# Index scores of a sparse-attention block: the low part of the keys in row halves of TensorE, two heads at a time

## The chip, the cores and the metric

The kernel runs on one core of a Trainium2 chip. The metric is the device time of one execution in microseconds, the median of three runs. The profile is one more execution, taken by the hardware profiler.

## The reference

A hybrid block on 2048 positions of width 1024: an input projection, an RWKV-7 recurrence as one branch, sparse attention as the other, both gated, merged and normed. The change touches the index scores of the sparse branch. For every query (in blocks of 128) 8 index heads of width 64 score all earlier keys, and the 256 best keys are kept:

```python
s_idx = jax.nn.relu(jnp.einsum('bqhd,bsd->bqhs', qi_b, ki))
score = jnp.einsum('bqh,bqhs->bqs', wi_b, s_idx).astype(jnp.float32)
score = jnp.where(causal[None], score, -jnp.inf)
_, sel = lax.top_k(score, topk)
```

The keys `ki` are the same for all heads; `wi` weighs the heads. The choice of keys has to be exact enough in float32, so the kernel works with numbers split in two: a high part `hi`, rounded to the form that TensorE multiplies, and a low part `lo`, the rest.

## The kernel before, in words

`build` (from L1207) states the stages in this order, each with a priority band (a smaller number goes first): `start` (norm and transposes), `gemm_index` (L277, index queries, keys and head weights), `select` (L372, index scores and choice of keys), `gemm_half` for the first two of four blocks of 512 tokens, then the recurrence (`rwkv_open`, `rwkv_pass`, `rwkv_inv`, `rwkv_chain`) with `gemm_half` for the other two blocks around it, `heads`, `branch_a`, `attention`, `finish`. A planner orders each engine's instructions ahead of time, with a simulated timeline: an instruction of a lower band is placed where nothing of a higher one is ready. So the products of `gemm_half` (all made at L251 by `unit`) fill TensorE between the score matmuls of `select`. On the chip each engine then takes its instructions in that fixed order.

`gemm_index` makes the index queries 128 rows (two heads) at a time. `split_out` (L255) writes their high and low parts, and `stacked` (L269) stores them by four transfers on SyncE's queue (issued at L75 by `move`) into `QIS`, an array of 8 heads by 128 rows: rows 0 to 63 of a head are its high part, rows 64 to 127 its low part. `stacked` is used for the attention queries `QS` too. The keys' two parts go to `KIH`.

`select` loads the keys into two tiles `kim`: `M[0]` holds the high part twice, in rows 0 to 63 and again in 64 to 127, and `M[1]` the low part twice. It goes through five groups of query blocks, (14, 15), (11, 12, 13), (8, 9, 10), (5, 6, 7), (2, 3, 4); blocks 0 and 1 need no choice. For each block it loads the queries of all heads as `st` (128 rows, 8 heads, 128 queries) and goes over the keys in chunks of at most 1024 columns and over the 8 heads. A head's scores for a chunk are a tile `ixs` of 128 by 1024, two banks of PSUM; there are three such tiles in turn. In cuts of at most 512 columns, two matmuls (L423) go into it: `st[:, h]` with `M[0]` and with `M[1]`. As `st` holds high and low one above the other, the two give (hi + lo) times the high keys and (hi + lo) times the low keys, all four products. Each matmul has its own weight load (the page calls the loads PEld). ScalarE then takes the tile out with a ReLU (L425, tile `re`, two of them) and VectorE adds it, weighed, to the block's scores (L429 for the first head, L431). Behind that, statistics and eight counting passes find the threshold (L434 to L471), and the mask goes to memory (L492 to L501).

After the choice of keys the recurrence begins. It has matmuls with operands of 64 rows, so of half the array's height: L654 and L659 (low part of two small weights, in rows 0 to 63 and 64 to 127, each right behind a whole one, L653 and L658) and L703 (four matmuls in the lower half of the rows, then four in the upper). Its last matmuls are those of L808.

Of the kernel before, what the change touches and what calls it, by code (L numbers as in the profile page):

```python
# [24 lines left out]
FT = mybir.dt.float32  # L25
# [26 lines left out]
class Block:  # L52
# [216 lines left out]
    def stacked(self, dst, p, m, tb, scale=None):  # L269
        DMA = self.nc.sync  # L270
        hi, lo = self.split_out(p, scale)
        s = slice(tb * TB, (tb + 1) * TB)
        for hh in range(2):
            self.move(dst[2 * m + hh, 0:64, s], hi[hh * 64:hh * 64 + 64])
            self.move(dst[2 * m + hh, 64:128, s], lo[hh * 64:hh * 64 + 64])

    def gemm_index(self):  # L277
        nc = self.nc
# [93 lines left out]
    def select(self):  # L372
# [7 lines left out]
        V, A, T, G, DMA = nc.vector, nc.scalar, nc.tensor, nc.gpsimd, nc.sync  # L380
        MID = TOPK - 4.0
        with ExitStack() as ctx:
            k1 = self.pool("ix1", 1, side="right", ctx=ctx)
            w = self.pool("ixw", 2, side="right", ctx=ctx)
            ps = self.pool("ixp", 3, PSUM, ctx=ctx)
            M = [k1.tile([128, S], FR, name=f"kim{i}") for i in range(2)]
# [13 lines left out]
            for grp in self.groups:  # L400
# [4 lines left out]
                def sm(name, n=4, dt=FT, bufs=2):  # L405
                    return w.tile([128, n], dt, name=name, bufs=bufs)

                s1, s2, t, cnt = sm("s1"), sm("s2"), sm("t", bufs=3), sm("cnt", bufs=3)
                mean, inv = sm("mean"), sm("inv")
                for g, qb in enumerate(grp):  # L410
                    n, n1 = 128 * (qb + 1), 128 * qb
                    st = w.tile([128, 8, 128], FR, name="st")
                    self.move(st, self.QIS[:, :, qb * 128:(qb + 1) * 128].rearrange("h p q -> p h q"))
                    sco = w.tile([128, S], FT, name="sc", bufs=6)
                    sc.append(sco)
                    for k0 in range(0, n, 1024):
                        kn = min(1024, n - k0)
                        for h in range(8):
                            p = ps.tile([128, 1024], FT, name="ixs")
                            for a in range(0, kn, 512):  # L420
                                b = min(a + 512, kn)
                                for i in range(2):
                                    T.matmul(p[:, a:b], st[:, h], M[i][:, k0 + a:k0 + b], start=i == 0, stop=i == 1)  # L423
                            r = w.tile([128, 1024], FT, name="re")
                            A.activation(r[:, :kn], p[:, :kn], AF.Relu)  # L425
                            wi = self.wi[:, qb, h:h + 1]
                            o = sco[:, k0:k0 + kn]
                            if h == 0:
                                V.tensor_scalar(o, r[:, :kn], wi, None, op0=OP.mult)  # L429
                            else:  # L430
                                V.scalar_tensor_tensor(o, r[:, :kn], wi, o, op0=OP.mult, op1=OP.add)  # L431
                    V.tensor_tensor(sco[:, n1:n], sco[:, n1:n], tri, op=OP.add)

                    j = w.tile([128, S], BF, name="ja", bufs=1)  # L434
                    A.activation(j[:, :n1], sco[:, :n1], AF.Copy, accum_out=s1[:, g:g + 1])
                    V.tensor_scalar(mean[:, g:g + 1], s1[:, g:g + 1], -1.0 / n1, None, op0=OP.mult)
                    j = w.tile([128, S], BF, name="ja", bufs=1)
                    A.activation(j[:, :n1], sco[:, :n1], AF.Abs, bias=mean[:, g:g + 1], accum_out=s2[:, g:g + 1])
                    V.scalar_tensor_tensor(t[:, g:g + 1], s2[:, g:g + 1], zc[:, qb, 0:1], mean[:, g:g + 1],
                                           op0=OP.mult, op1=OP.subtract)  # L440
                    V.tensor_tensor(inv[:, g:g + 1], s2[:, g:g + 1], zc[:, qb, 1:2], op=OP.mult)
                hs = [w.tile([128, S], BF, name="hs", bufs=4) for _ in grp]
                told = cold = None
                for it in range(self.passes):
                    if it:
# [15 lines left out]
                        told, cold, t, cnt = t, cnt, tn, sm("cnt", bufs=3)  # L461
# [16 lines left out]
                p = ps.tile([128, 1024], FT, name="ixs")  # L478
# [898 lines left out]
```

## Time and profile before

| | |
|---|---|
| median of three runs | 2543.67 us |
| the three runs | 2540.09, 2543.67, 2544.42 us |
| the profiled execution | 2535.82 us |
| its span, first to last instruction | 2534.0 us |
| mean granted TensorE clock | 0.987 |
| TensorE matmuls busy | 2414.3 us (95%) |
| TensorE weight loads busy | 2134.6 us (84%) |
| VectorE, ScalarE, GpSimd busy | 1615.2, 1235.3, 804.8 us |

Times in the profile count from the span's start. PE is TensorE's matmuls, PEld its weight loads, which run beside the matmuls; DVE is VectorE, ACT ScalarE, POOL GpSimd, SP SyncE. A matmul's duration holds the way through the array, so matmuls overlap, and what one costs is read from start to start. "128\*128 128x512" is a weight of 128 rows by 128 columns and a moving operand of 128 rows by 512 columns. "Idle before" is the time in which the engine stood still ahead of an instruction; "issue" as its cause means that no semaphore of another engine explains it. The index scores and the choice of keys lie between 215 and 840 us.

### The profile page before, as it was taken

Reading aid. Unit: us, or ns where it says so; the run is one execution under the profiler, and the core shown is the slowest. Engines: PE = TensorE matmul, PEld = TensorE weight load, DVE = VectorE, ACT = ScalarE, POOL = GpSimd, SP = SyncE. Lnnn points to the kernel's source line nnn. Section 1 sums busy time; section 2 is a strip of 40 time slices with the busy share of each in tenths; the row PEclk is TensorE's granted clock in tenths of the full one; section 3 lists DMA queues with packets and bytes.
Section 4 is the critical chain, followed back from the end, with each engine's and each line's share of the span. In section 5 each row is a group of like instructions: output and inputs, shape, how many; then the busy total and the mean of one; then the engine's idle time right before and its main releaser. Section 6 shows DMA issues by size and latency. Waiting matters only on the chain.

```text
span 2534.0 us, 44949 instructions
## 1 busy us (share of the span) xinstructions
PE 2414.3 (95%) x16776; PEld 2134.6 (84%) x16776; DVE 1615.2 (64%) x3381; ACT 1235.3 (49%) x2024; POOL 804.8 (32%) x694
## 2 busy tenths in 40 slices
PE   4899999999999999999999999999889999989998
PEld 3687878888888998889888989989779999988887
DVE  6614778776877556654936757344478888876443
ACT  4414646555544424334434333352478888865332
POOL 2411111111121333233333332131255555544332
PEclk9999999999999999999999999999999999999999
DMA  7754223423336556777677769978753343155442
GB/s 248 280 152 125 89 83 92 125 96 96 104 98 217 147 164 193 191 203 225 194 206 212 214 188 276 298 240 250 232 166 87 91 118 99 29 182 192 142 150 71
DMA packets 423496, 415.67 MB, mean 164 GB/s; under 512 B 80010, under 2 KB 339890, under 8 KB 418404
## 3 DMA queue, kind: packets, MB, share of 16 engines
q1 hardware_dynamic: 422692, 404.33, 53.1%
q0 software_dynamic: 576, 8.39, 0.8%
q8 instruction: 132, 2.16, 0.4%
q14 instruction: 96, 0.79, 0.1%
HBM read 254.04 MB, written 160.15 MB: 163 GB/s over the span
## 4 chain that ended last, share of the span: by engine, by line
PE 49%; DMA 7%; DVE 5%; issue 3%; ACT 2%; SPq 2%; POOL 2%; POOLq 0%; ACTq 0%; DVEq 0%
PE g L251 16%; PE fo L1196 6%; PE yv L993 4%; PE br L1111 4%; PE pt L976 3%; PE pg L703 2%; PE lg L959 2%; PE lg L960 2%; DMA xt<-in_w_pb_dram 1%; PE pp L808 1%; PE pp L791 1%; PE zu L797 1%; PE hp L801 1%; PE pp L788 1%; DVE prd L740 1%
## 5 line engine op out<-in xcount | busy, mean ns | idle before, releaser
L251 PE MATMUL g<-hh,whi 128*128 128x256 f32 (+1 forms) x2176 | 718.9, 330 | 8.8 <-DVE eo L265 4.7
L251 PE MATMUL g<-hl,whi 128*128 128x256 f32 (+1 forms) x2176 | 715.3, 329 | 2.9 <-POOL hl L169 2.9
L251 PE MATMUL g<-hh,wlo 128*128 128x256 f32 (+1 forms) x2176 | 714.9, 329 | 1.4 <-POOL wlo L237 1.4
L237 POOL TENSOR_TENSOR wlo<-wraw,whi 128x1024 fp32r<-128x1024 f32 (+1 forms) x89 | 225.1, 2529 | 748.3 <-ACT whi L236 695.0
L251 PEld LDWEIGHTS g<-hh,whi 128*128 128x128 f32 x2176 | 416.0, 191 | 54.7 <-issue 6.5
L251 PEld LDWEIGHTS g<-hl,whi 128*128 128x128 f32 x2176 | 416.2, 191 | 43.4 <-issue 4.1
L251 PEld LDWEIGHTS g<-hh,wlo 128*128 128x128 f32 x2176 | 416.0, 191 | 41.7 <-issue 4.3
L431 DVE SCALAR_TENSOR_TENSOR sc<-re,wi,sc 128x1024 f32<-128x1024 f32 (+7 forms) x154 | 170.7, 1108 | 56.7 <-ACT re L425 50.8
L425 ACT ACTIVATE re<-ixs 128x1024 f32<-128x1024 f32 (+7 forms) x176 | 140.4, 816 | 135.5 <-PE ixs L423 78.7
L236 ACT CAST whi<-wraw 128x1024 fp32r<-128x1024 f32 (+1 forms) x89 | 92.8, 1043 | 174.2 <-PE g L251 132.3
L976 PE MATMUL pt<-ident,lt 128*128 128x128 f32 x1088 | 168.1, 275 | 7.0 <-ACT tp L982 4.3
L966 ACT ACTIVATE lt<-lt,nm 128x128 f32<-128x128 f32 (+15 forms) x128 | 154.8, 1212 | 15.3 <-DVE nm L965 15.2
L987 DVE TENSOR_TENSOR pl<-pt,ph 128x512 fp32r<-128x512 f32 (+1 forms) x216 | 139.0, 657 | 31.6 <-ACT ph L986 30.7
L423 PE MATMUL ixs<-kim,st 128*128 128x512 f32 (+3 forms) x608 | 150.2, 373 | 8.3 <-ACT re L425 4.8
L962 DVE CUSTOM_DVE_ANT_0 lt<-lg,mask 128x512 f32<-128x512 f32 (+3 forms) x256 | 147.4, 589 | 16.5 <-PE lg L960 9.0
L993 PE MATMUL yv<-ph,vp 128*128 128x256 f32 (+1 forms) x576 | 152.1, 285 | 5.7 <-ACT ph L986 5.6
L993 PE MATMUL yv<-pl,vp 128*128 128x256 f32 x576 | 153.0, 301 | 2.0 <-POOL pl L984 1.8
L959 PE MATMUL lg<-m,sq 128*128 128x256 f32 (+3 forms) x384 | 136.6, 365 | 5.9 <-DMA mask<-mask 4.1
L423 PEld LDWEIGHTS ixs<-kim,st 128*128 128x128 f32 x608 | 113.1, 190 | 34.5 <-ACT re L425 6.9
L976 PEld LDWEIGHTS pt<-ident,lt 128*128 128x128 f32 x1088 | 125.7, 141 | 16.9 <-ACT tp L982 5.3
L986 ACT CAST ph<-pt 128x512 fp32r<-128x512 f32 (+1 forms) x216 | 116.4, 564 | 20.8 <-PE pt L976 14.3
L960 PE MATMUL lg<-m,sq 128*128 128x256 f32 (+3 forms) x384 | 126.2, 336 | 0.0
(343 smaller groups left out, 5106.6 us busy)
## 6 DMA issues: line engine op xcount, KB each, us to landing
wraw<-in_w_in_dram SPq DMA_DIRECT2D x88, 512.0 KB
gg<-eo SPq DMA_DIRECT2D x64, 256.0 KB
gmd<-gt SPq DMA_DIRECT2D x64, 256.0 KB
gmc<-gmd SPq DMA_DIRECT2D x32, 512.0 KB
g<-gg SPq DMA_DIRECT2D x64, 256.0 KB
m<-ks SPq DMA_DIRECT2D x32, 512.0 KB
pj<-eo SPq DMA_DIRECT2D x52, 256.0 KB
x<-in_ada_w_dram SPq DMA_DIRECT2D x24, 512.0 KB
```

The costliest lines, as they stand in the source:

```text
L237: nc.gpsimd.tensor_tensor(lo[:, :, :n], raw[:, :, :n], hi[:, :, :n].bitcast(FT), op=OP.subtract)
L251: T.matmul(p[:, s], a[:, k], b[:, k, s], start=n == 0, stop=n == 3 * KD - 1)
L423: T.matmul(p[:, a:b], st[:, h], M[i][:, k0 + a:k0 + b], start=i == 0, stop=i == 1)
L425: A.activation(r[:, :kn], p[:, :kn], AF.Relu)
L431: V.scalar_tensor_tensor(o, r[:, :kn], wi, o, op0=OP.mult, op1=OP.add)
L959: T.matmul(p[:, :kn], sq[:, qb * 128:(qb + 1) * 128], m1[:, k0:k1_], start=True, stop=False)
L960: T.matmul(p[:, :kn], sq[:, qb * 128:(qb + 1) * 128], m2[:, k0:k1_], start=False, stop=True)
L962: V.tensor_tensor_reduce(lt[:, k0:k1_], p[:, :kn], mk, 1.0, -3.0e38, OP.subtract, OP.max, cm[:, i:i + 1])
L966: ex = A.activation(lt[:, :n], lt[:, :n], AF.Exp, bias=nm, accum_out=lsum[:, qb, h:h + 1])
L976: T.transpose(p[:, o:o + 128], L[i][:, kt * 128:(kt + 1) * 128], self.ident)
L993: T.matmul(yv[:, qs], vp[:, kt, :], b[:, o:o + nn], start=kt == 0 and i == 0, stop=kt == last and i == 1, skip_group_check=True)
L1196: T.matmul(p, a[:, k, q], b[:, k, s], start=n == 0, stop=n == 23)
```

## The change

`stacked` stores odd heads of `QIS` with the low part in rows 0 to 63 and the high part in rows 64 to 127; even heads, and `QS`, are as before. `select` takes two heads at a time and two tiles `ixs` at once. First come the whole passes with the high keys, for the one head over all cuts, then for the other. Then, cut by cut, each head's high queries with the low keys, 64 rows: rows 0 to 63 for the even head, rows 64 to 127 for the odd one. The product of low with low is no longer made. ReLU and the weighed sum are unchanged.

```diff
         hi, lo = self.split_out(p, scale)
         s = slice(tb * TB, (tb + 1) * TB)
         for hh in range(2):
-            self.move(dst[2 * m + hh, 0:64, s], hi[hh * 64:hh * 64 + 64])
-            self.move(dst[2 * m + hh, 64:128, s], lo[hh * 64:hh * 64 + 64])
+            for i, t in enumerate((hi, lo)):
+
+                o = 64 * (i ^ (hh if dst is self.QIS else 0))
+                self.move(dst[2 * m + hh, o:o + 64, s], t[hh * 64:hh * 64 + 64])
...
                     for k0 in range(0, n, 1024):
                         kn = min(1024, n - k0)
+                        cuts = [(a, min(a + 512, kn)) for a in range(0, kn, 512)]
                         for h in range(8):
-                            p = ps.tile([128, 1024], FT, name="ixs")
-                            for a in range(0, kn, 512):
-                                b = min(a + 512, kn)
-                                for i in range(2):
-                                    T.matmul(p[:, a:b], st[:, h], M[i][:, k0 + a:k0 + b], start=i == 0, stop=i == 1)
+                            if h % 2 == 0:
+
+                                pp = [ps.tile([128, 1024], FT, name="ixs") for i in range(2)]
+                                for i, p in enumerate(pp):
+                                    for a, b in cuts:
+                                        T.matmul(p[:, a:b], st[:, h + i], M[0][:, k0 + a:k0 + b], start=True, stop=False)
+                                for a, b in cuts:
+                                    for i, p in enumerate(pp):
+                                        r_ = slice(i * 64, i * 64 + 64)
+                                        T.matmul(p[:, a:b], st[r_, h + i], M[1][r_, k0 + a:k0 + b], start=False, stop=True)
+                            p = pp[h % 2]
                             r = w.tile([128, 1024], FT, name="re")
```

## Rows read from the trace of the kernel before

**Rows 1.** The page, busy time of each engine in the whole span.
```profile
PE 2414.3 (95%) x16776; PEld 2134.6 (84%) x16776; DVE 1615.2 (64%) x3381; ACT 1235.3 (49%) x2024; POOL 804.8 (32%) x694
```

**Rows 2.** Busy time by stretch, index stage; columns as in its first line.
```profile
core 0: us, PE busy (x) PEld busy (x) DVE busy (x) ACT busy (x) POOL busy (x), PEclk, DMA share, GB/s
215.00:830.00 615.00, 607.31 (x2802) 502.92 (x2803) 467.78 (x932) 329.70 (x446) 107.70 (x42) 0.99 0.35 109
```

**Rows 3.** The chain that ended last, 764 to 795 us: start, duration, what.
```profile
765.23 3.45 PE g L251 x15
768.68 0.46 PE ixs L423 x2
769.14 1.83 PE g L251 x8
...
784.94 0.63 PE ixs L423 x4
785.57 2.34 PE g L251 x10
```

**Rows 4.** Waits between 215 and 830 us: in total, times, longest.
```profile
ACT re L425 <- PE ixs L423: 78.7, 53, 4.9
DVE sc L431 <- ACT re L425: 50.8, 48, 3.3
...
PE ixs L423 <- ACT re L425: 4.8, 3, 2.9
```

**Rows 5.** Groups of instructions by shape, TensorE, L423: count, busy us, mean ns.
```profile
L423 PE MATMUL ixs<-kim,st 128*128 128x512 f32 x448 | 126.4, 401 | 8.2 <-ACT re L425 4.8 <-DMA st<-qis 3.4
L423 PE MATMUL ixs<-kim,st 128*128 128x384 f32 x64 | 15.9, 342 | 0.1
L423 PE MATMUL ixs<-kim,st 128*128 128x256 f32 x48 | 9.6, 282 | 0.0
L423 PE MATMUL ixs<-kim,st 128*128 128x128 f32 x48 | 8.0, 248 | 0.0
```

**Rows 6.** Timeline of weight loads: start us, us, two runs of L423.
```profile
400.13 1.80 PEld L423 LDWEIGHTS ixs<-kim,st 128*128 128x128 f32 x8
...
405.65 2.92 PEld L423 LDWEIGHTS ixs<-kim,st 128*128 128x128 f32 x16
```

**Rows 7.** Timeline of matmuls: two of 256 columns in a run.
```profile
1111.09 0.28 PE L251 MATMUL g<-hh,whi 128*128 128x256 f32 x1
1111.21 0.28 PE L251 MATMUL g<-hl,whi 128*128 128x256 f32 x1
```

**Rows 8.** Timeline of weight loads: a block of half height.
```profile
898.09 0.96 PEld L703 LDWEIGHTS pg<-ar,bk 64*128 64x128 f32 x8
```

**Rows 9.** Timeline of matmuls: one of half height between whole ones.
```profile
1497.03 0.39 PE L653 MATMUL pg<-sw,w2s 128*128 128x512 f32 x1
1497.35 0.49 PE L654 MATMUL pg<-sw,wa2l 64*128 64x512 f32 x1
1497.77 0.39 PE L251 MATMUL g<-hl,whi 128*128 128x256 f32 x1
1498.00 0.28 PE L251 MATMUL g<-hh,wlo 128*128 128x256 f32 x1
```

**Rows 10.** Timeline of weight loads at the same place.
```profile
1496.92 0.19 PEld L653 LDWEIGHTS pg<-sw,w2s 128*128 128x128 f32 x1
1497.35 0.18 PEld L654 LDWEIGHTS pg<-sw,wa2l 64*128 64x128 f32 x1 [0.24 <-issue]
1497.77 0.19 PEld L251 LDWEIGHTS g<-hl,whi 128*128 128x128 f32 x1 [0.24 <-issue]
```

**Rows 11.** Timeline of matmuls around the block of rows 8.
```profile
897.88 0.28 PE L251 MATMUL g<-hh,wlo 128*128 128x256 f32 x1
898.09 1.16 PE L703 MATMUL pg<-ar,bk 64*128 64x128 f32 x8
899.17 0.39 PE L251 MATMUL g<-hh,whi 128*128 128x256 f32 x1
899.40 0.28 PE L251 MATMUL g<-hl,whi 128*128 128x256 f32 x1
```

**Rows 12.** DMA issues: queue, count, KB each.
```profile
qis<-eo SPq DMA_DIRECT2D x64, 128.0 KB
```

**Rows 13.** Busy time by stretch, columns as in rows 2.
```profile
1100.00:1150.00 50.00, 50.00 (x522) 45.30 (x522) 21.64 (x35) 15.82 (x29) 17.84 (x18) 1.00 0.72 212
```

**Rows 14.** Groups by shape, VectorE and ScalarE, one head of 1024 columns.
```profile
L431 DVE SCALAR_TENSOR_TENSOR sc<-re,wi,sc 128x1024 f32<-128x1024 f32 x70 | 94.3, 1348 | 23.4 <-ACT re L425 20.6
L425 ACT ACTIVATE re<-ixs 128x1024 f32<-128x1024 f32 x80 | 80.5, 1026 | 66.0 <-PE ixs L423 42.6 <-DVE sc L431 12.5 <-DVE sc L429 7.6
```

**Rows 15.** One line's instructions: ns min/median/max, first and last start us.
```profile
L251 PE MATMUL g<-hh,wlo x2176: 274/283/632, 44.8 to 1693.4; 128*128 128x256 f32 x122, 128*128 128x512 f32 x76
L808 PE MATMUL pp<-uv,gmc x512: 222/222/310, 1113.6 to 1717.2; 128*64 128x64 f32 x171
```

**Rows 16.** Busy time by stretch: 800 to 900 and 1000 to 1100 us.
```profile
800.00:850.00 50.00, 46.95 (x387) 46.33 (x387) 36.10 (x142) 15.67 (x25) 13.63 (x16) 1.00 0.63 196
...
sum 200.00, PE 185.94 PEld 174.40 DVE 134.67 ACT 78.09 POOL 62.65; mean PE 46.48 PEld 43.60 DVE 33.67 ACT 19.52 POOL 15.66
```

## The prediction

> **What bounds the kernel now.** I read the page's busy times first: TensorE is busy 2414.3 of the 2534.0 us, its weight loads 2134.6, and VectorE, the next engine, 1615.2 [rows 1]. So TensorE is the bound unless the stage of the change says otherwise. That stage lies between 215 and 830 us: there TensorE is busy 607.3 of 615 us, VectorE 467.8, and the granted clock is 0.99, the higher level (2.4 GHz) [rows 2]. It is full because the planner puts the projection products of L251 between the scores: the chain that ended last runs in this stretch from one to the other, a few score matmuls of L423, then a run of L251, and each costs about 0.23 us per 512 columns (15 in 3.45 us, 2 in 0.46) [rows 3]. The waits say the same from the other side: TensorE waited 4.8 us in all for a score buffer, while ScalarE waited 78.7 us for scores and VectorE 50.8 us for ScalarE's result [rows 4]. Those engines have slack; a microsecond more or less in TensorE's queue moves everything behind it. I therefore count the change in TensorE time and treat the passage to the end as one to one, with the exceptions as rivals.
>
> **What the index scores cost now.** There are 608 matmuls of L423: 448 of 512 columns, 64 of 384, 48 of 256 and 48 of 128 [rows 5]. Each column cut takes 16 of them (8 heads by 2), so there are 28, 4, 3 and 3 cuts. Times from start to start: for 512 columns, 8 weight loads in a row take 1.80 us, the last 0.19, so (1.80 - 0.19)/7 = 0.23 us; where 512 and 128 alternate, 16 loads take 2.92 us, so a couple takes (2.92 - 0.19)/15 x 2 = 0.364, leaving 0.13 for 128 columns [rows 6]. For 384, four in 0.63 us gives 0.16 [rows 3]. For 256 the nearest row is L251's, 0.12 [rows 7].
>
> **What the change removes.** In a pair of heads four passes per cut become two whole ones and two of half height. If the two halves run side by side they last as long as one, but two weight loads still have to be made, and those of 64 rows by 128 columns follow at (0.96 - 0.19)/7 = 0.11 us [rows 8], so a side-by-side couple takes no less than 0.22. Saved per pair and cut: 512 columns 0.46 - 0.23 = 0.23; 384: 0.32 - 0.22 = 0.10; 256: 0.24 - 0.22 = 0.02; 128: 0.26 - 0.22 = 0.04. Over four pairs: 28 x 4 x 0.23 = 25.8, 4 x 4 x 0.10 = 1.6, 12 x 0.02 = 0.2, 12 x 0.04 = 0.5, **28.1 us** together.
>
> No row shows two row halves at work at once. The bounds are the couple's 0.23 us (side by side) and 0.46 (one after the other, nothing saved). I take side by side: in the block of L703 the row half changes after the fourth of eight matmuls and the loads keep their 0.11 us through it, so the second half is loaded without waiting for the first to empty [rows 8]. The row doesn't decide it, because a stream of 128 columns is shorter than a load; it only shows no penalty. The choice sets the size of the forecast and not its sign.
>
> **What the change adds: two switches of height per pair.** The trace has this step elsewhere. At 1497.03 a whole matmul of 512 columns starts (L653), at 1497.35 one of half height (L654), at 1497.77 a whole one of 256 and at 1498.00 the next [rows 9]. From the first start to the last is 0.97 us; without switches it would be 0.23 + 0.23 + 0.12 = 0.58. So the way there and back costs 0.39 us. The load queue shows where it goes: between whole matmuls the next load starts with the matmul ahead of it, but L654's load comes 0.32 us after L653 started, and L251's 0.42 us after that, each after 0.24 us of idle time for which no other engine is named [rows 10]. The load waits until the array has emptied, and then lies open. A second place gives the same: around eight half-height matmuls (L703), 897.88 to 899.40 is 1.52 us, against 0.12 + 8 x 0.11 + 0.12 = 1.12 [rows 8, 11]. I take **0.40 us per pair and chunk**.
>
> The blocks 2 to 15 have chunks of up to 1024 columns: one each for blocks 2 to 7, two each for 8 to 15, 22 in all, so 88 pairs: 88 x 0.40 = 35.2 us. On top, the second half of a couple starts one load later than the first and ends later by as much: 0.11 by the row [rows 8], at best 0 if both loads go at once: 0 to 9.7 us. I take 9.7, because the row shows loads of the two row halves following one another at 0.11 us. The Trainium skill (TensorE: Matmul & The Clock Gate, Part 3) models packed tiles as starting some 4 ns apart; by it this term would be nearly nothing and the sum about 7 us instead of 17. No run here shows such a start.
>
> **What moves at no cost.** The head queries are stored with low parts first for odd heads: still 64 transfers of 128 KB [rows 12] in the same issue order, only their rows in memory differ, so nothing passes anything else on SyncE's queue. The products have as many instructions as before (608), and lo by lo is dropped. The granted clock is 1.00 in 1100 to 1150 us too, where blocks of half height stand (L703 among them), so I keep it [rows 13].
>
> **What is held longer.** A pair holds two of the three score buffers until both are done. The first head's scores come later by the second's whole passes (0.46), the switch and the halves, over 1 us; after ScalarE frees the buffer for the second head of the next pair, TensorE needs about 0.46 + 0.2 + 0.66 = 1.3 us until that pair is ready, and VectorE has one head of 1.35 us left to work on [rows 14]. It just fits if no run of L251 stands between, so VectorE will wait more. It was already idle 147 of 615 us [rows 2], TensorE's time is filled with L251, and the later recurrence can absorb little: L251 ends at 1693 us and the chain's last matmuls at 1717 us [rows 15]. I price this at 0 and leave up to 10 us above it for the range.
>
> **Sum.** 35.2 + 9.7 - 28.1 = +16.8 us. The profiled execution took 2535.82 us (span 2534.0), 7.85 below the median of the runs, 2543.67; the difference is carried to the median: 2543.67 + 16.8 = **2560.5 us**, 0.7% slower. With simultaneous loads it is +7.1, 2550.8; with 10 us of late scores 2570. A difference of 0.2% (5 us) is about what a measurement tells from none.
>
> **Rivals.**
> 1. *The halves don't overlap* (slower). Then nothing is saved and the switches stay: +35.2, 2579, or up to 2589 with late scores. For it: no row shows an overlap. Against: nothing waits at the row halves' border in L703 [rows 8].
> 2. *The switch is nearly free when both row halves are loaded* (faster). In the two places of the trace part of the array stood empty, or the halves came from one source; perhaps a couple that fills all rows lets the next whole load through. The saving would win as soon as the round trip costs less than (28.1 - 9.7)/88 = 0.21 us. At no cost: -18.4 to -28.1, so 2515 to 2525. Against: both places give 0.40, and L703 had used both row halves [rows 11]. By the Trainium skill (TensorEngine Tiling, Key Properties) changing the tiling mode, though not changing the tile, drains TensorE; that lowers this rival's chance, and the trace agrees with its 0.40 us.
> 3. *TensorE's extra time is swallowed* (no change). In the stretches 800 to 900 and 1000 to 1100 us TensorE is idle for 200 - 185.9 = 14 us, behind weight transfers and the recurrence's first inverse [rows 16]. If that serial path, and not TensorE, sets the time from there, up to 14 of the 17 us vanish: about 2546. Against: the chain before it is made of L251 and L423 [rows 3], and the path starts only when selection ends, which isn't earlier.
>
> **How the numbers follow.** Forecast 0.52, halves one after the other 0.16, cheap switch 0.15, swallowed 0.17. The forecast's own range is 2550 to 2571. To hold 8 in 10 it goes down past the swallowed case, to 2538, and up over most of rival 1, to 2586; the cheap switch (0.15) and the last part of rival 1 stay out. Faster: rival 2 and a little for a new order by the planner, 0.17. Same: rival 3 and a small part of the forecast's low end, 0.20. Slower: the rest, 0.63.
>
> **What would show it.** L423 should have 304 matmuls of 128 rows and 304 of 64. In a 1024 chunk the pair (4 whole, 4 half) should take about 1.9 us against 1.84 for 8 whole now, with a gap of some 0.24 us ahead of the first half-height load and of the next whole one. If half-height matmuls of one couple start 0.11 us apart and the couples 0.23, the overlap is real; if all start 0.23 apart, rival 1 holds. If the loads at the switches show no gap, rival 2. L251's last start should go from 1693 to about 1710 us; if it does and the end doesn't move, or the idle time at 800 to 1100 shrinks by as much, rival 3. The forecast is wrong if the round trip costs under 0.32 us, where the saving breaks even without the load term.

## The result and the profile after

The changed kernel takes 2617.94 us (median of 5 runs, 2616.22 to 2626.82) against 2543.67: a ratio of 1.0314, 95% interval 1.0296 to 1.0332. That is 74 us more where 17 were forecast, and outside the range. The profiled execution took 2617.94 us with a span of 2616.1.

The page's first part, for [rows 1]:

```profile
PE 2492.1 (95%) x16776; PEld 2133.0 (82%) x16776; DVE 1598.9 (61%) x3381; ACT 1233.8 (47%) x2020; POOL 795.6 (30%) x694
```

TensorE is as full as before and for 78 us longer, with the same number of instructions and no more time in weight loads. So no instruction was added; the matmuls count as running for longer. The index stage by stretch, for [rows 2] (columns as there):

```profile
215.00:830.00 615.00, 612.29 (x2459) 438.84 (x2460) 426.03 (x792) 309.83 (x403) 99.36 (x39) 0.99 0.30 90
```

In the same 615 us TensorE gets through 2459 matmuls in place of 2802, at the same clock. The timeline of its matmuls shows where (start us, us, engine, line, operation, count):

```profile
227.15 0.62 PE L427 MATMUL ixs<-kim,st 128*128 128x512 f32 x2
227.70 0.73 PE L431 MATMUL ixs<-kim,st 64*128 64x512 f32 x2
228.37 0.73 PE L427 MATMUL ixs<-kim,st 128*128 128x512 f32 x2
229.03 0.73 PE L431 MATMUL ixs<-kim,st 64*128 64x512 f32 x2
229.68 0.50 PE L251 MATMUL g<-hl,whi 128*128 128x512 f32 x1
```

L427 are the whole passes, L431 those of half height. Two whole ones and two halves, then the next two and two: that is one head at a time, not four whole and four half per pair. From 228.37 to 229.68 one head takes 1.31 us; four matmuls in a row are 4 x 0.23 = 0.92. The round trip costs 0.39 us, as in [rows 9], but each *head* pays it here. The load queue at this place, for [rows 10]:

```profile
227.70 0.29 PEld L431 LDWEIGHTS ixs<-kim,st 64*128 64x128 f32 x2 [0.36 <-issue]
228.37 0.30 PEld L427 LDWEIGHTS ixs<-kim,st 128*128 128x128 f32 x2 [0.37 <-issue]
229.03 0.29 PEld L431 LDWEIGHTS ixs<-kim,st 64*128 64x128 f32 x2 [0.36 <-issue]
```

Ahead of each change of height shown here the loads stand still for about 0.36 us with no other engine to wait for. Such a gap is not the price itself: matmuls still run during part of it, and the price is read from start to start. Over the stage, the waits of the load queue and of the engines behind it (in total, times, longest; the last two answer to [rows 4], all between 215 and 850 us, where the kernel before has the same 78.7 and 50.8 us as in its shorter stretch):

```profile
PEld ixs L431 <- issue: 50.9, 162, 0.7
PEld g L251 <- issue: 32.8, 110, 0.4
PEld ixs L427 <- issue: 12.8, 29, 3.8
...
ACT re L434 <- PE ixs L431: 151.8, 98, 6.7
DVE sc L440 <- ACT re L434: 103.3, 66, 6.4
```

162 gaps ahead of half-height loads, where 88 were forecast; in TensorE's order there are 167 runs of L431. Only 12 of them hold both heads. One that does, from the timeline:

```profile
352.26 1.20 PE L427 MATMUL ixs<-kim,st 128*128 128x512 f32 x4
353.39 0.73 PE L431 MATMUL ixs<-kim,st 64*128 64x512 f32 x4
354.05 0.50 PE L251 MATMUL g<-hl,whi 128*128 128x512 f32 x1
...
418.08 0.73 PE L431 MATMUL ixs<-kim,st 64*128 64x512 f32 x2
```

Four halves in two row halves take 0.73 us, no more than two in one row half at 418. The overlap that the change is built on is real, and here the additional loads cost nothing. It just seldom happens. The first pair of all, when the three score tiles were still free, also stayed together. Later, tiles come free one at a time, at the pace of the engines behind. My reading is that the planner then has everything for the first head, whole passes and halves, while the second head still waits for its tile, and that it places what is ready. No run tests this reason by itself; what the order shows is that the program's order within a pair doesn't bind the planner.

How the delay travels: the last ReLU of the scores, the last mask of the selection, the last products of L251 and the last matmuls of the recurrence (ns min/median/max, first and last start us; L251 and L817 answer to [rows 15]):

```profile
L434 ACT ACTIVATE re<-ixs x176: 268/920/1052, 218.4 to 852.4; 128x1024 f32<-128x1024 f32 x80, 128x896 f32<-128x896 f32 x16, 128x512 f32<-128x512 f32 x16, 128x640 f32<-128x640 f32 x16
L509 ACT ACTIVATE mk<-y,big x14: 617/1311/2004, 369.7 to 910.5; 128x1920 bf16<-128x1920 f32 x1, 128x2048 bf16<-128x2048 f32 x1, 128x1536 bf16<-128x1536 f32 x1, 128x1664 bf16<-128x1664 f32 x1
L251 PE MATMUL g<-hh,wlo x2176: 274/283/632, 45.3 to 1760.7; 128*128 128x256 f32 x122, 128*128 128x512 f32 x76
L817 PE MATMUL pp<-uv,gmc x512: 222/222/369, 1186.0 to 1798.9; 128*64 128x64 f32 x171
```

In the kernel before, the first two were:

```profile
L425 ACT ACTIVATE re<-ixs x176: 258/921/1042, 217.1 to 791.1; 128x1024 f32<-128x1024 f32 x80, 128x896 f32<-128x896 f32 x16, 128x512 f32<-128x512 f32 x16, 128x640 f32<-128x640 f32 x16
L500 ACT ACTIVATE mk<-y,big x14: 617/1310/2002, 355.2 to 839.9; 128x1920 bf16<-128x1920 f32 x1, 128x2048 bf16<-128x2048 f32 x1, 128x1536 bf16<-128x1536 f32 x1, 128x1664 bf16<-128x1664 f32 x1
```

The scores end 61 us late, the selection 71, L251 67, the recurrence 82, and the span ends 82 late (82 and not 74, because the profiled execution of the kernel before was 8 us below its median). So 71 of the 82 us are there when the selection ends and the recurrence begins; the rest is added in the recurrence, and nothing later swallows it.

### The profile page after: what moved, and what is told of

It reads as the page before. It is cut to its first block, busy times and chain, and to the rows that moved or that the text cites. A ratio compares the mean times of both kernels' runs of the same rounds, so it can differ in the third digit from the quotient of the medians.

```text
span 2616.1 us, 44950 instructions
## 1 busy us (share of the span) xinstructions
PE 2492.1 (95%) x16776; PEld 2133.0 (82%) x16776; DVE 1598.9 (61%) x3381; ACT 1233.8 (47%) x2020; POOL 795.6 (30%) x694
## 4 chain that ended last, share of the span: by engine, by line
PE 49%; DMA 6%; DVE 5%; issue 3%; ACT 2%; POOL 1%; SPq 1%; POOLq 0%; ACTq 0%; DVEq 0%
PE g L251 14%; PE fo L1205 5%; PE yv L1002 4%; PE br L1120 4%; PE pt L985 3%; PE pg L712 2%; PE lg L968 2%; PE lg L969 2%; PE zu L806 1%; PE pp L817 1%; PE pp L800 1%; PE pp L797 1%; PE hp L810 1%; DMA xt<-in_w_pb_dram 1%; DVE tm L751 1%
## 5 line engine op out<-in xcount | busy, mean ns | idle before, releaser
L251 PE MATMUL g<-hh,whi 128*128 128x256 f32 (+1 forms) x2176 | 724.8, 333 | 6.4 <-DVE prev L341 2.6
L251 PE MATMUL g<-hl,whi 128*128 128x256 f32 (+1 forms) x2176 | 723.0, 332 | 2.8 <-POOL hl L169 2.4
L251 PE MATMUL g<-hh,wlo 128*128 128x256 f32 (+1 forms) x2176 | 720.7, 331 | 0.2 <-POOL wlo L237 0.2
L251 PEld LDWEIGHTS g<-hh,whi 128*128 128x128 f32 x2176 | 418.0, 192 | 61.4 <-issue 15.5
L251 PEld LDWEIGHTS g<-hl,whi 128*128 128x128 f32 x2176 | 418.2, 192 | 56.3 <-issue 17.2
L237 POOL TENSOR_TENSOR wlo<-wraw,whi 128x1024 fp32r<-128x1024 f32 (+1 forms) x89 | 219.1, 2462 | 790.9 <-ACT whi L236 706.3
L251 PEld LDWEIGHTS g<-hh,wlo 128*128 128x128 f32 x2176 | 417.8, 192 | 48.5 <-issue 13.1
L996 DVE TENSOR_TENSOR pl<-pt,ph 128x512 fp32r<-128x512 f32 (+1 forms) x216 | 139.0, 656 | 35.6 <-ACT ph L995 35.2
L1002 PEld LDWEIGHTS yv<-ph,vp 128*128 128x128 f32 x576 | 110.6, 193 | 17.3 <-ACT ph L995 7.4
L1002 PEld LDWEIGHTS yv<-pl,vp 128*128 128x128 f32 x576 | 110.0, 192 | 8.1 <-POOL pl L993 4.1
```

The costliest lines, as they stand in the source:

```text
L237: nc.gpsimd.tensor_tensor(lo[:, :, :n], raw[:, :, :n], hi[:, :, :n].bitcast(FT), op=OP.subtract)
L251: T.matmul(p[:, s], a[:, k], b[:, k, s], start=n == 0, stop=n == 3 * KD - 1)
L996: V.tensor_tensor(pl[:, :n], p[:, :n], ph[:, :n].bitcast(FT), op=OP.subtract)
L1002: T.matmul(yv[:, qs], vp[:, kt, :], b[:, o:o + nn], start=kt == 0 and i == 0, stop=kt == last and i == 1, skip_group_check=True)
```

## The experiments

Two theories stood at the start. S: the planner split the pairs, so that about 170 switches are paid and almost nothing is saved. L: a pair holds two of three score tiles, which makes scores, selection and the recurrence late. Each run was timed against the kernel before on the same chip.

**Pairs held together.** The halves are queued behind the pair's last whole pass.

```diff
-                                        T.matmul(p[:, a:b], st[:, h + i], M[0][:, k0 + a:k0 + b], start=True, stop=False)
-                                for a, b in cuts:
+                                        mm = T.matmul(p[:, a:b], st[:, h + i], M[0][:, k0 + a:k0 + b], start=True, stop=False)
+                                with tc.issue_after(mm.ins):
+                                    for a, b in cuts:
...
```

> The changed kernel, with one thing added: the half-height matmuls of a pair are queued behind the last whole pass of the second head, so that the planner can't put one head's halves behind that head's own whole passes. 88 runs of half height in place of 167, all 304 in couples of both row halves. Theory S (the planner split the pairs, so nearly each head pays its own switch of about 0.40 us and nearly no couple runs side by side): 88 x 0.40 - 28.1 = +7, 2551 us, between 2543 and 2561. Rival L (a pair holds two of the three score tiles, scores come late, selection and the recurrence start late): the tiles are held as long or longer here, so it stays at 2590 or above.

2655.65 us against 2541.83, ratio 1.0453 (1.0435 to 1.0470). S's number falls, L's holds: with 88 gaps and every couple side by side it is slower still. The gaps ahead of the half-height loads, the ReLUs and L251 of this run:

```profile
PEld ixs L432 <- issue: 26.9, 88, 0.7
L435 ACT ACTIVATE re<-ixs x176: 268/917/1030, 216.9 to 930.9; 128x1024 f32<-128x1024 f32 x80, 128x896 f32<-128x896 f32 x16, 128x512 f32<-128x512 f32 x16, 128x640 f32<-128x640 f32 x16
L251 PE MATMUL g<-hh,wlo x2176: 274/283/628, 44.5 to 1548.0; 128*128 128x256 f32 x122, 128*128 128x512 f32 x76
```

The scores end at 930.9 us and the selection at 986.7, 147 us late, but L251 ends at 1548, 145 us *earlier* than before. While the selection waits, TensorE goes on with L251, and then has none left to fill the recurrence. By stretch, this run and then the kernel before:

```profile
1100.00:1700.00 600.00, 570.82 (x4973) 513.12 (x4972) 343.03 (x618) 203.47 (x339) 188.19 (x176) 0.89 0.67 195
1700.00:1900.00 200.00, 171.38 (x1447) 152.42 (x1444) 91.75 (x166) 73.26 (x129) 33.45 (x38) 0.85 0.88 273
```

```profile
1100.00:1700.00 600.00, 596.85 (x5822) 541.90 (x5821) 337.09 (x607) 230.75 (x390) 185.05 (x182) 1.00 0.78 229
1700.00:1900.00 200.00, 174.86 (x1364) 165.31 (x1365) 106.77 (x279) 95.01 (x178) 67.30 (x70) 0.96 0.70 212
```

Between 1100 and 1700 us TensorE makes 4973 matmuls in place of 5822, with idle time, and in part at the lower of its two clock levels, 1.2 GHz: the granted clock is 0.89 on average against 1.00, and 0.62 from 1550 to 1700 us, when L251 has ended and TensorE is busy for only 129 of 150 us.

**Pairs, all passes whole.**

```diff
-                                        r_ = slice(i * 64, i * 64 + 64)
-                                        T.matmul(p[:, a:b], st[r_, h + i], M[1][r_, k0 + a:k0 + b], start=False, stop=True)
+                                        T.matmul(p[:, a:b], st[:, h + i], M[1][:, k0 + a:k0 + b], start=False, stop=True)
```

> Two heads and two tiles at a time as in the changed kernel, but the pass with the low keys is whole again (128 rows, lo by lo included), so there is no switch and no saving. Theory S: no change against the kernel before, 2544 us within 10. Rival L: two tiles are held just the same, so 2585 or above.

2562.15 us, ratio 1.0077 (1.0057 to 1.0097): +20, between the two. So taking two heads at a time has a price of its own where the planner may still split them, but a small one.

This run is also the exact counterpart of the changed kernel: in the two traces the instructions of TensorE, of ScalarE and of VectorE stand in the same order from first to last, so the planner parts the pairs in the same 167 places whatever the height. The place shown above from 228.37 to 229.68:

```profile
228.07 0.63 PE L427 MATMUL ixs<-kim,st 128*128 128x512 f32 x2
228.53 0.63 PE L430 MATMUL ixs<-kim,st 128*128 128x512 f32 x2
229.00 0.39 PE L251 MATMUL g<-hl,whi 128*128 128x512 f32 x1
```

Here the head takes 0.93 us, in the changed kernel 1.31. The two kernels differ by 1.0314 against 1.0077, some 60 us (56 between the medians), and only the height differs between them: that is what 167 switches cost, less what the few couples save.

Its waits between 215 and 850 us:

```profile
ACT re L433 <- PE ixs L430: 95.8, 54, 6.2
DVE sc L439 <- ACT re L433: 56.9, 49, 4.1
```

95.8 and 56.9 us against 78.7 and 50.8 [rows 4]: the engines behind wait a little more. The last ReLU starts 6 us later than before (796.8) and the last mask of the selection 15 us later (854.7), so most of the 20 us is there when the selection ends.

**One head at a time, second pass of half height.**

```diff
                             for a in range(0, kn, 512):
                                 b = min(a + 512, kn)
-                                for i in range(2):
-                                    T.matmul(p[:, a:b], st[:, h], M[i][:, k0 + a:k0 + b], start=i == 0, stop=i == 1)
+                                T.matmul(p[:, a:b], st[:, h], M[0][:, k0 + a:k0 + b], start=True, stop=False)
+                            for a in range(0, kn, 512):
+                                b = min(a + 512, kn)
+                                T.matmul(p[:, a:b], st[0:64, h], M[1][0:64, k0 + a:k0 + b], start=False, stop=True)
```

> The kernel before, one head and one tile at a time, where only the pass with the low keys is cut to 64 rows (rows 0 to 63, high queries by low keys; lo by lo is dropped). No pair, no row half beside another. Theory S: 176 round trips of 0.40 us and nothing saved: +70, 2614 us, between 2600 and 2632. Rival L: the tiles are held as before, so within 10 us of the kernel before.

2604.94 us, ratio 1.0251 (1.0234 to 1.0268): +63.1, with tiles and heads as before. L alone falls here: switches make the kernel slower without any pair. 63.1/176 = 0.36 us per round trip. The load queue's waits from 215 to 860 us:

```profile
PEld ixs L425 <- issue: 54.3, 176, 0.7
PEld g L251 <- issue: 36.8, 122, 0.7
PEld ixs L422 <- issue: 11.7, 28, 2.8
```

The sum, the count and the places are nearly those of the changed kernel (50.9, 32.8 and 12.8 us).

**Pairs held, both halves in the same rows.** Queries of all heads lie high part first, and both halves use rows 0 to 63.

```diff
-                o = 64 * (i ^ (hh if dst is self.QIS else 0))
+                o = 64 * i
...
-                                            r_ = slice(i * 64, i * 64 + 64)
+                                            r_ = slice(0, 64)
```

> As the held pairs, but both heads' high queries lie in rows 0 to 63 and both halves use those rows, so they can't run side by side; the number of runs of half height is 88 again. Theory S: the switches alone, 88 x 0.40 = +35, 2579 us, 28 more than the held pairs in separate row halves. If row halves don't overlap, or the overlap is worth nothing, this equals the held pairs within 5 us.

2686.69 us, ratio 1.0567 (1.0541 to 1.0592). The level was wrong, as in the first run, but the difference is the point: 31.0 us more than the held pairs, where 28 were expected, with TensorE's instructions in the same order. That is what the overlap is worth. A block of four halves of 512 columns in this run, and in the held pairs:

```profile
277.49 1.20 PE L432 MATMUL ixs<-kim,st 64*128 64x512 f32 x4
278.62 0.72 PE L427 MATMUL ixs<-kim,st 128*128 128x512 f32 x2
```

```profile
269.26 0.73 PE L432 MATMUL ixs<-kim,st 64*128 64x512 f32 x4
269.93 0.73 PE L427 MATMUL ixs<-kim,st 128*128 128x512 f32 x2
```

From the first half to the next whole pass it is 1.13 us in one row half and 0.67 side by side: 0.46 less for two couples, so 0.23 for each, as forecast. The timeline names only the shape of a block's first matmul; by the start of each matmul, couples of 384, 256 and 128 columns save 0.18, 0.11 and 0.10 us (0.55, 0.43 and 0.36 in one row half against 0.37, 0.32 and 0.26). Over all 152 couples that is 31 us, the measured difference.

**Pairs held, all passes whole.** The first run's order, without switches.

```diff
-                                            r_ = slice(i * 64, i * 64 + 64)
-                                            T.matmul(p[:, a:b], st[r_, h + i], M[1][r_, k0 + a:k0 + b], start=False, stop=True)
+                                            T.matmul(p[:, a:b], st[:, h + i], M[1][:, k0 + a:k0 + b], start=False, stop=True)
```

> As the held pairs (the second pass of a pair queued behind the last first pass of its second head), but every pass is whole: no switch, no row halves, lo by lo included. The held pairs took 114 us more than before; their 88 switches at 0.36 (63.1/176 from the single heads) are 32 us, and the overlap gave back 31 (against the same row half). Theory L2 (holding a pair together makes the scores late, and that is nearly the whole of the 114): 2655 us within 15. Rival M (the lateness needs the switches too): about the pairs of whole passes, 2562, below 2600.

2654.07 us, ratio 1.0425 (1.0385 to 1.0465): L2's number within a microsecond. The instructions stand in the order of the held pairs, so holding the pair together costs 110 us by itself; with halves, 88 switches (32) and the overlap (31) cancel.

**One head at a time, a half pass behind each whole one.** The second loop over the cuts is taken out of the third run, so each cut switches.

```diff
                                 T.matmul(p[:, a:b], st[:, h], M[0][:, k0 + a:k0 + b], start=True, stop=False)
-                            for a in range(0, kn, 512):
-                                b = min(a + 512, kn)
                                 T.matmul(p[:, a:b], st[0:64, h], M[1][0:64, k0 + a:k0 + b], start=False, stop=True)
```

> The kernel before, one head and one tile at a time, where a half-height pass follows each whole pass cut by cut: 304 runs of half height in place of 176, the same 304 half-height matmuls. Lo by lo is dropped. Theory S (the price goes by the switch): 304 x 0.36 = +109, 2651 us, between 2635 and 2665. Rival P (a half-height pass costs more by itself, however many switches): as the single heads before, 2605 within 8.

2657.35 us, ratio 1.0444 (1.0407 to 1.0481): +113.1, or 0.37 us for each of 304, with the instructions of TensorE, ScalarE and VectorE in the order of the kernel before. The price goes by the switch; P falls.

**Score tiles of one bank.** Six tiles of 512 columns in place of three of 1024; first one head at a time.

```diff
-            ps = self.pool("ixp", 3, PSUM, ctx=ctx)
+            ps = self.pool("ixp", 6, PSUM, ctx=ctx)
...
-                    for k0 in range(0, n, 1024):
-                        kn = min(1024, n - k0)
+                    for k0 in range(0, n, 512):
+                        kn = min(512, n - k0)
...
-                            p = ps.tile([128, 1024], FT, name="ixs")
+                            p = ps.tile([128, 512], FT, name="ixs")
...
-                            r = w.tile([128, 1024], FT, name="re")
+                            r = w.tile([128, 512], FT, name="re", bufs=4)
```

> The kernel before with score tiles of one bank: chunks of 512 columns, six tiles in turn, four ReLU tiles; all passes whole, one head at a time. 128 more instructions each on ScalarE and VectorE, on VectorE 2 x 0.87 us in place of 1.35 per 1024 columns. It is the base for the next run. All theories: between 2530 and 2580.

2574.61 us, ratio 1.0117 (1.0081 to 1.0152), the base for two runs. Next, the same tiles with held pairs and halves:

> Score tiles of one bank, six in turn, chunks of 512 columns; pairs held together, 152 runs of half height, each one couple in both row halves. Against the narrow tiles with whole passes: theory S with L2 (a pair now holds two of six tiles, so scores aren't late): 152 x 0.36 - 31 = +24, between +12 and +36. If pairs make scores late however many tiles there are: +70 or more.

2604.04 us, ratio 1.0217 (1.0178 to 1.0256): 29 above the base, within S with L2. The last mask of the selection starts at 852 us, 38 later than in the base (814), where the held pairs with three tiles were 147 later than the kernel before. And the same tiles with pairs of whole passes, not held:

> Score tiles of one bank, six in turn, and pairs of heads whose passes are all whole: no switch, no row halves. It tells what the 20 us of the pairs of whole passes with three tiles come from. Theory L3 (two of three tiles held make scores late): with two of six there is nothing left, so within 8 us of the narrow tiles with one head at a time, 2575. Rival O (the new order by the planner costs it, whatever the tiles): 15 or more above that, 2590.

2572.79 us, ratio 1.0127 (1.0108 to 1.0146) against 1.0117 for the base: no difference. With six tiles of half the width a pair costs nothing (its selection even ends 9 us earlier than the base's, at 805), and L3 holds: this fits that the 20 us of the second run, and most of the 110 of the fifth, come from holding two tiles of three. It doesn't separate the number of tiles from their width: a pair of narrow tiles also holds its buffers for half as many passes. And six tiles don't keep the pairs together by themselves: in this run's order only 24 of 152 pairs have their two second passes next to each other.

**The same price elsewhere: whole rows in the kernel before.** The kernel before has 222 runs below whole height in the planned order, most of them in the recurrence. Three versions of the kernel before fill some of them up with zero rows. First the one-hot matmuls (the tiles of 40 rows get 128, which the writes that zeroed the 40 now cover):

```diff
-        R["oneht"] = c1.tile([40, 4, 128], FR, name="oneht")
+        R["oneht"] = c1.tile([128, 4, 128], FR, name="oneht")
...
-        R["nr"] = c1.tile([40, 512], FR, name="nrs")
+        R["nr"] = c1.tile([128, 512], FR, name="nrs")
...
-            ohr = k1.tile([40, 4, 128], FR, name="ohr")
+            ohr = k1.tile([128, 4, 128], FR, name="ohr")
```

> The kernel before, with another use of the same price: the one-hot matmuls of 40 rows (L674 and L1047) get their operands filled with zero rows up to 128, so they no longer switch the height. The planned order has 204 runs of less than whole height in place of 222. Theory S: 18 x 0.36 to 0.40 = -7 us, 2537, between 2532 and 2544. Rival N (in the recurrence the switches stand where TensorE waits anyhow): no change within 3 us.

2538.44 us against 2542.10, ratio 0.9980 (0.9965 to 0.9995, 5 rounds): 5 us faster by the ratio (1 to 9 by its interval), against 7 expected, and a small step below both kernels. That leans to S; N's "no change within 3 us" is not excluded. Then with the chain's matmuls too:

```diff
-            ttc = ch.tile([64, 8, 64], FT, name="ttc")
+            ttc = ch.tile([128, 8, 64], FT, name="ttc")
...
+            G.memset(ttc[64:128], 0.0)
+            G.memset(uv[0:64], 0.0)
...
-                T.matmul(pp[0:64, h * 64:h * 64 + 64], gmc[64:128, h, 0:64], uv[64:128, h * 64:h * 64 + 64],
+                T.matmul(pp[0:64, h * 64:h * 64 + 64], gmc[:, h, 0:64], uv[:, h * 64:h * 64 + 64],
...
-            xx = ch.tile([64, 512], FT, name="xx", bufs=1)
-            A.copy(xx, pp[0:64])
+            xx = ch.tile([128, 512], FT, name="xx", bufs=1)
+            A.copy(xx, pp)
```

> The same, and the 64-row matmuls of the recurrence's chain (L791 and L797) made whole too: zero rows in ttc and uv, written by GpSimd once per chunk, and xx copied in 128 rows. 148 runs of less than whole height in place of 222. Theory S: 74 x 0.36 to 0.40 = -27 to -30, 2515 us, between 2508 and 2528. Rival N (the switches stand in waits of the chain, or the chain and not TensorE sets the time there, and the zero rows cost GpSimd time on it): between 2537 and 2555.

2548.18 us, ratio 1.0021 (1.0011 to 1.0032): N holds. From the groups between 1100 and 1750 us:

```profile
L770 POOL MEMSET ttc<- 64x512 f32 x30 | 15.8, 525 | 1.3
L771 POOL MEMSET uv<- 64x512 f32 x30 | 15.5, 517 | 62.7 <-PE pp L810 55.2 <-DVE prd L740 4.5 <-issue 2.9
```

Zeroing `uv` waits 55 us in all for earlier chunks' matmuls, and what GpSimd has to do for the chain is queued behind it. Without that write (the last diff without the lines on `uv` and `gmc`):

> The kernel before with the one-hot matmuls in 128 rows as in the first such version, and of the chain's matmuls only L797 made whole (zero rows in ttc, written by GpSimd; xx copied in 128 rows); no zero rows in uv, whose write waited 55 us in the last version and held GpSimd's queue. 172 runs of less than whole height in place of 222. Theory S: 50 x 0.36 = -18, 2524 us, between 2516 and 2532. Rival N (the chain's switches stand in its waits, or the zero rows delay it): no better than the one-hot version, 2534 to 2545.

2556.30 us, ratio 1.0051 (1.0034 to 1.0068). So that wait wasn't the reason, or not the only one. Why 32 fewer switches in the chain make it slower is left open. What the three show is that the price of 0.36 us can't simply be booked as a gain in the recurrence; that other engines set the pace there is a guess that no run settles.

## Why the prediction was wrong

*The price of a switch* was right: 0.40 us from two places of the trace, 0.36 and 0.37 from the runs of one head at a time. The Trainium skill (TensorEngine Tiling, Key Properties) says that a change of tiling mode drains TensorE; the gaps of 0.36 us ahead of the loads agree.

*The count of switches failed:* "22 in all, so 88 pairs" took the program's order for the chip's. The planner parted nearly all pairs, so that each head paid. There were 167 runs of half height, 167 x 0.36 = 60 us in place of 35.2.

*The saving failed with it.* The choice "side by side" was right, and 31.0 us for all couples is close to the 28.1 of the sum. But only 12 of the 167 runs held couples, 19 in all: 19 x 0.23 = 4 us at most, in place of 28.1.

*The load term* of 9.7 us was wrong: it is 0, as four halves take as long as two. In the held pairs' trace the two halves of a couple start at 269.262 and 269.266 us; the eight matmuls of L703, from which the term was taken, change the row half only once. The floor of 0.22 us per couple, also taken from those loads, fell too: couples of 384, 256 and 128 columns save 0.18, 0.11 and 0.10 us where 0.10, 0.02 and 0.04 were booked. The Trainium skill's model (TensorE: Matmul & The Clock Gate, Part 3) has packed tiles start some 4 ns apart; the trace agrees with its 0.004 us.

*What is held longer* was priced at 0, with 10 us above. It is 20 (pairs of whole passes, in the same order). The prediction saw the mechanism: a pair holds two tiles of three, and a new pair needs 1.3 us where VectorE has 1.35 left. It didn't draw the other conclusion from it, that a planner which fills gaps would then part the pair.

With the measured terms the sum is 60 - 4 + 20 = 76 us; the measured change is 74. The first two terms also come out of one comparison, the changed kernel against the pairs of whole passes in the same order: 56 to 60 us. Rival 1 (no overlap, 2579) came nearer the number than the forecast, for another reason: the halves can overlap, but they weren't given the chance. Rival 2 is out: the switch was never cheap, not even between couples that fill all rows (88 gaps in the held pairs, which are no faster than the same order with whole passes). Rival 3 is out: L251 and the end moved with the index stage.

## What to carry to other kernels

Running two half-height matmuls side by side saves half their time, but going to half height and back costs as much as 1.6 passes of 512 columns (0.36 / 0.23), so by these figures a run of halves must hold at least two such couples to gain anything; with 152 couples in 88 runs, gain and price cancelled. Count these runs in the order that the engine gets, not in the program's: here the planner parted most pairs that need two buffers at once, and its order was the same whether a pass had 64 or 128 rows. Where they are forced together, look at what the held buffers do to the engines behind and at how the filler work is used up.

## What the runs showed that was not expected

Four half-height matmuls of 512 columns with four loads, in two row halves, take the same 0.67 us to the next whole one as two in one row half. And late scores show in TensorE's time not in the stage where they are late: in the held pairs the filler ended 145 us early, and TensorE then lost its time in the recurrence behind it, with idle time and at a mean granted clock of 0.89 between 1100 and 1700 us.
